# Splitting one late output store by partitions, so that eight DMA engines carry more of it than the other eight

## The chip, the cores and the metric

One Trainium2 chip, one of its cores. The metric is the device time of one execution in microseconds; the kernel before has a median of 211.49 us over five runs (210.92 to 213.69).

## What is computed

```python
batch, m, k, n = 16, 512, 1024, 768
# x: (16, 512, 1024), weight: (1024, 768), sub_value: (16, 512, 768), all float32
def reference(x, weight, sub_value):
    return (np.matmul(x, weight) - sub_value).astype(np.float32)
```

One matrix product of 8192 rows by 1024 by 768, from which a matrix of the output's shape is subtracted. In float32 the core reads 33.6 MB of `x`, 25.2 MB of `sub_value` and 3.1 MB of weights, and writes 25.2 MB.

## The kernel before, in words

**Tiling.** The 8192 rows are 64 tiles of 128 rows (`mi` from 0 to 63). Eight tiles make a superblock of 1024 rows in which partition `p` holds eight neighbouring rows (L56 to L58). So a transfer of `n` tiles is, in every one of 128 partitions, one run that is contiguous in HBM and in SBUF: n x 4096 bytes for `x`, n x 3072 bytes for `sub_value` and the output.

**Rings.** `x_ring` holds 16 tiles of `x`; `so_ring` holds 32 tiles of `sub_value`. The result of a tile is written over its `sub_value` tile in the same slot, and the store reads it there.

**Work on a tile.** ScalarE casts `x` to float16 (`cast`, L134 or L131). Of most tiles TensorE makes the transposes (L143) and ScalarE copies them out of PSUM (L150); of ten pairs of tiles VectorE does the transposes instead (L164). TensorE then does 16 matmuls of 128x384 (L176). VectorE subtracts (`finish`, L188) and writes `so_ring`.

**Order of the transfers.** All transfers are issued by SyncE (SP), on one queue, in the order of the list `TRANSFERS` (L23 to L30), written by hand. An entry is a kind (`x`, `w`, `s` for sub_value, `o` for output), a first tile and a number of tiles. `issue()` (L90) is called after every cast and every finish; it takes the next entry off the list when what it needs is done, and stops at the first that has to wait. A store `('o', at, n)` needs `finish` of all its tiles. At the end of the list of the kernel before stand six stores in a row: `('o', 32, 8)`, `('o', 40, 8)`, `('o', 48, 8)`, `('o', 56, 5)`, `('o', 61, 2)`, `('o', 63, 1)` behind the last load `('s', 56, 8)`; the last three of them finish the output.

**The code that the change touches.** One line issues a store, L119, and one a load, L121; each of them is one DMA over all 128 partitions:

```python
            here = ring[:, at % size : at % size + n]
            there = view[at // S][:, at % S : at % S + n]
            if kind == "o":
                keep(nc.sync.dma_start(out=there, in_=here))
```

Each DMA is spread over the core's 16 DMA engines, and raises its completion semaphore once for each engine that took part. The program ends (L287) when SP has seen all completions.

Of the kernel before, what the change touches and what calls it, by code (L numbers as in the profile page):

```python
# [8 lines left out]
P = 128  # L9
# [16 lines left out]
    ('x', 16, 2), ('x', 18, 6), ('s', 16, 8), ('x', 24, 8), ('s', 24, 8), ('x', 32, 8),  # L26
    ('o', 0, 8), ('x', 40, 8), ('s', 32, 8), ('o', 8, 8), ('o', 16, 8), ('s', 40, 8),
    ('x', 48, 8), ('o', 24, 8), ('s', 48, 8), ('x', 56, 8), ('s', 56, 8), ('o', 32, 8),
    ('o', 40, 8), ('o', 48, 8), ('o', 56, 5), ('o', 61, 2), ('o', 63, 1),
]  # L30


@with_exitstack
def kernel(
# [7 lines left out]
    nc = tc.nc  # L42
    keep = tc.keep_in_program_order
# [46 lines left out]
    def issue():  # L90
        while todo:
            kind, at, n = todo[0]
            span = set(range(at, at + n))
            old = {t - NX if kind == "x" else t - NSO for t in span}
            need, by = {
                "w": (set(), "o"),
                "x": ({t for t in old if t >= 0}, "cast"),
                "s": ({t for t in old if t >= 0}, "o"),
                "o": (span, "finish"),
            }[kind]  # L100
            if not need <= done[by]:
                return
            todo.pop(0)
            done[kind] |= span
            if kind == "w":

                first = NSO - 2 * (n_c - at)
                st = so_ring[:, first : first + 2]
                keep(nc.sync.dma_start(out=st, in_=w_c[at]))  # L109
                for r in range(2):  # L110
                    keep(nc.vector.tensor_copy(out=w_sb[:, at, r], in_=st[:, r]))  # L111
                continue
            ring, size, view = {
                "x": (x_ring, NX, x_s), "s": (so_ring, NSO, sub_s), "o": (so_ring, NSO, out_s)
            }[kind]
            here = ring[:, at % size : at % size + n]
            there = view[at // S][:, at % S : at % S + n]
            if kind == "o":
                keep(nc.sync.dma_start(out=there, in_=here))  # L119
            else:  # L120
                keep(nc.sync.dma_start(out=here, in_=there))  # L121

    def cast(mi):
        assert mi in done["x"]
        done["cast"].add(mi)
        x_in = x_ring[:, mi % NX]
        first = mi - mi % 2
        if first in ON_DVE:
            if mi == first:
                x16_t["pair", mi] = x16p_pool.tile([P, 2, K], F16, name="x16p_tile")  # L130
            keep(nc.scalar.copy(out=x16_t["pair", first][:, mi - first], in_=x_in))  # L131
        else:
            x16_t[mi] = x16_pool.tile([P, K], F16, name="x16_tile")
            keep(nc.scalar.copy(out=x16_t[mi], in_=x_in))  # L134
        issue()
# [48 lines left out]
    def finish(mi):  # L184
        assert mi in done["s"]
        done["finish"].add(mi)
        o = so_ring[:, mi % NSO].rearrange("p (h n) -> p h n", h=2)
        keep(nc.vector.tensor_tensor(  # L188
            out=o, in0=po_t.pop(mi)[:, :, :NS], in1=o, op=mybir.AluOpType.subtract
        ))  # L190
        issue()

    issue()


# [96 lines left out]
```

## Time and profile before

| | |
|---|---|
| median of five runs | 211.49 us (210.92 to 213.69) |
| the profiled execution | 211.42 us; its span in the profile 209.6 us |
| granted TensorE clock, mean | 0.983 |
| PE busy | 195.6 us (93%) |
| DVE busy | 134.5 us (64%) |
| ACT busy | 106.7 us (51%) |
| data queue (q1) | 5040 packets, 87.03 MB, 97.6% of 16 engines' span |
| last matmul ends, last subtraction ends | 202.0 us, 203.0 us |
| the last three stores are issued at | 194.66, 200.40 and 203.00 us |

How to read it: the span runs from the first to the last instruction that the profiler recorded; the execution's own time has 1.8 us more. All times inside the profile are counted from the start of the span. A packet is one run of one transfer on one DMA engine, or the 4-byte write with which an engine reports that its share of a transfer is done; 35 transfers x 16 engines give 560 such reports, and these are the 560 packets under 512 bytes. Two other queues carry no data of the kernel: q8 and q14 are of the kind "instruction".

### The profile page before, as it was taken

How to read it: one execution, taken by the hardware profiler on the slowest of the kernel's cores; microseconds unless marked ns; L12 is line 12 of the kernel's file. 1: busy time of each engine (PE TensorE's matmuls, PEld its weight loads, DVE VectorE, ACT ScalarE, POOL GpSimd, SP SyncE). 2: the span in 40 equal slices, each digit the busy share in tenths (PEclk: the TensorE clock that was granted, in tenths of full speed). 3: DMA queues.
4: the chain of work that ended last, by engine and by line, in shares of the span. 5: the costliest groups of instructions: out<-in, count | busy, mean ns of one | idle time of the engine just before them, and what ended most of it. 6: DMA issues, size and time to landing. Idle time of an engine off the chain costs nothing.

```text
span 209.6 us, 2950 instructions
## 1 busy us (share of the span) xinstructions
PE 195.6 (93%) x1225; PEld 127.5 (61%) x1225; DVE 134.5 (64%) x234; ACT 106.7 (51%) x109; POOL 0.7 (0%) x6
## 2 busy tenths in 40 slices
PE   7589699999999999999999999999999999999950
PEld 3246366766766666666666666666665656776620
DVE  0131332489999965999838999995398994332330
ACT  3353847938282537554464917350955243755300
POOL 1000000000000000000000000000000000000000
PEclk9969999999999999999999999999999999999996
DMA  6999999999999999999999999999999999999993
GB/s 217 423 444 424 434 421 422 450 425 430 422 464 411 417 444 439 413 428 452 411 424 431 427 435 427 441 414 419 422 441 441 435 411 427 431 439 422 424 407 131
DMA packets 5052, 87.21 MB, mean 416 GB/s; under 512 B 560, under 2 KB 560, under 8 KB 1456
## 3 DMA queue, kind: packets, MB, share of 16 engines
q1 hardware_dynamic: 5040, 87.03, 97.6%
q8 instruction: 9, 0.15, 0.3%
q14 instruction: 3, 0.02, 0.0%
HBM read 61.87 MB, written 25.17 MB: 415 GB/s over the span
## 4 chain that ended last, share of the span: by engine, by line
PE 80%; DMA 10%; DVE 5%; SPq 1%; issue 0%; DVEq 0%
PE psum_o L176 72%; DMA so_ring<-in_sub_value_dram 10%; PE psum_t L143 8%; DVE xtp_tile L164 3%; DVE so_ring L188 2%; SPq L109 1%; SPq L121 1%; DVEq L188 0%
## 5 line engine op out<-in xcount | busy, mean ns | idle before, releaser
L176 PE MATMUL psum_o<-w_sb,xt_tile 128*128 128x384 f16 x704 | 125.5, 327 | 1.7 <-DVE so_ring L188 1.7
L176 PEld LDWEIGHTS <-xt_tile 128*128 128x128 f16 x704 | 68.9, 98 | 40.0 <-issue 2.8
L188 DVE TENSOR_TENSOR so_ring<-psum_o,so_ring 128x768 f32<-128x768 f32 x64 | 60.8, 957 | 43.9 <-PE psum_o L176 27.6
L150 ACT COPY xt_tile<-psum_t 128x1024 f16<-128x1024 f16 x44 | 44.5, 1012 | 75.4 <-PE psum_t L143 74.8
L164 DVE STREAM_TRANSPOSE xtp_tile<-x16p_tile 32x256 f32<-32x256 f32 x160 | 69.7, 436 | 12.1 <-ACT x16p_tile L131 9.6
L176 PE MATMUL psum_o<-w_sb,xtp_tile 128*128 128x384 f16 x320 | 61.3, 326 | 0.3 <-DVE xtp_tile L164 0.2
L134 ACT CAST x_tile<-x_ring 128x1024 f16<-128x1024 f32 x44 | 45.6, 1047 | 8.2 <-DMA x_ring<-in_x_dram 8.2
L143 PE MATMUL psum_t<-ident,x_tile 128*128 128x128 f32 x176 | 46.1, 277 | 3.2 <-ACT x_tile L134 3.0
L176 PEld LDWEIGHTS <-xtp_tile 128*128 128x128 f16 x320 | 31.2, 98 | 14.7 <-DVE xtp_tile L164 1.0
L143 PEld LDWEIGHTS psum_t<-ident,x_tile 128*128 128x128 f32 x176 | 24.5, 142 | 14.7 <-ACT x_tile L134 3.8
L131 ACT CAST x16p_tile<-x_ring 128x1024 f16<-128x1024 f32 x20 | 20.9, 1046 | 6.9 <-DMA x_ring<-in_x_dram 6.9
L111 DVE CAST w_sb<-so_ring 128x768 f16<-128x768 f32 x8 | 4.1, 556 | 11.6 <-DMA so_ring<-in_weight_dram 11.6
L204 PE MATMUL psum_o<-idle_x,idle_w 128*128 128x512 f16 x25 | 8.5, 492 | 1.3 <-DVE idle_x L199 1.3
L204 PEld LDWEIGHTS <-idle_w 128*128 128x128 f16 x25 | 3.0, 120 | 4.7 <-issue 2.9
L134 ACT ACT_TABLE_LOAD x1 | 1.3, 1283 | 0.7 <-PEq L276 0.7
L198 DVE MEMSET idle_w<- 128x64 uint32 x1 | 0.1, 112 | 0.8 <-PEq L276 0.8
masks.py:199 POOL TENSOR_SCALAR_AFFINE_SELECT ident<-ident 128x128 f32<-128x128 f32 x1 | 0.3, 292 | 0.1
L199 DVE MEMSET idle_x<- 128x256 uint32 x1 | 0.3, 272 | 0.0
masks.py:197 POOL MEMSET ident<- 128x128 f32 x1 | 0.2, 206 | 0.3 <-POOLq L276 0.3
L276 POOL MEMSET const-uint8-127<- 128x1 uint8 x1 | 0.1, 102 | 0.0
L276 POOL MEMSET const-bfloat16-1.0<- 128x1 bf16 x1 | 0.1, 101 | 0.0
L276 POOL MEMSET const-float32-0.0<- 128x1 f32 x1 | 0.1, 98 | 0.2 <-issue 0.2
(1 smaller groups left out, 0.1 us busy)
## 6 DMA issues: line engine op xcount, KB each, us to landing
so_ring<-in_sub_value_dram SPq DMA_DIRECT2D x7, 3072.0 KB, 27.4
out_dram<-so_ring SPq DMA_DIRECT2D x7, 3072.0 KB, 30.6
x_ring<-in_x_dram SPq DMA_DIRECT2D x5, 4096.0 KB, 20.5
so_ring<-in_weight_dram SPq DMA_DIRECT2D x4, 768.0 KB, 10.7
x_ring<-in_x_dram SPq DMA_DIRECT2D x2, 1536.0 KB, 18.6
so_ring<-in_sub_value_dram SPq DMA_DIRECT2D x2, 1536.0 KB, 24.5
x_ring<-in_x_dram SPq DMA_DIRECT2D x1, 3072.0 KB, 25.2
x_ring<-in_x_dram SPq DMA_DIRECT2D x1, 2560.0 KB, 26.9
```

The costliest lines, as they stand in the source:

```text
L109: keep(nc.sync.dma_start(out=st, in_=w_c[at]))
L111: keep(nc.vector.tensor_copy(out=w_sb[:, at, r], in_=st[:, r]))
L121: keep(nc.sync.dma_start(out=here, in_=there))
L131: keep(nc.scalar.copy(out=x16_t["pair", first][:, mi - first], in_=x_in))
L134: keep(nc.scalar.copy(out=x16_t[mi], in_=x_in))
L143: keep(nc.tensor.transpose(ps_t[mi].bitcast(F32)[:, c * P : (c + 1) * P], x16_t[mi].bitcast(F32)[:, c * P : (c + 1) * P], ident,))
L150: keep(nc.scalar.copy(out=xt_t[mi], in_=ps_t.pop(mi)))
L164: keep(nc.vector.transpose(xt[b * Q : (b + 1) * Q, :, a * Q : (a + 1) * Q], x16[a * Q : (a + 1) * Q, :, b * Q : (b + 1) * Q],))
L176: keep(nc.tensor.matmul(po_t[mi][:, h, :NS], xt_t[mi][:, 2 * P * c + r : 2 * P * (c + 1) : 2], w_sb[:, c, r, h * NS : (h + 1) * NS], start ...
L188: keep(nc.vector.tensor_tensor(out=o, in0=po_t.pop(mi)[:, :, :NS], in1=o, op=mybir.AluOpType.subtract))
L204: keep(nc.tensor.matmul(idle_o[:, 0], idle_w, idle_x, start=True, stop=True))
L276: nc = _bacc.Bacc("TRN2", target_bir_lowering=False, num_devices=1)
```

## The change

The third last store takes four tiles instead of five, and an additional store takes the fifth with its neighbour: five, two and one tiles become four, two, one and one. The store of four tiles is issued as four DMAs, one after the other, over partitions 0 to 63, 64 to 71, 72 to 79, and 80 to 127. All other transfers stay single DMAs over 128 partitions. By the description that comes with the change, the first eight DMA engines carry nine runs of this store, the others seven.

```diff
     ('x', 48, 8), ('o', 24, 8), ('s', 48, 8), ('x', 56, 8), ('s', 56, 8), ('o', 32, 8),
-    ('o', 40, 8), ('o', 48, 8), ('o', 56, 5), ('o', 61, 2), ('o', 63, 1),
+    ('o', 40, 8), ('o', 48, 8), ('o', 56, 4), ('o', 60, 2), ('o', 62, 1), ('o', 63, 1),
 ]
+
+SPLIT = ('o', 56)
+PARTS = ((0, 64), (64, 72), (72, 80), (80, 128))
...
             here = ring[:, at % size : at % size + n]
             there = view[at // S][:, at % S : at % S + n]
-            if kind == "o":
-                keep(nc.sync.dma_start(out=there, in_=here))
-            else:
-                keep(nc.sync.dma_start(out=here, in_=there))
+            for lo, hi in PARTS if (kind, at) == SPLIT else ((0, P),):
+                if kind == "o":
+                    keep(nc.sync.dma_start(out=there[lo:hi], in_=here[lo:hi]))
+                else:
+                    keep(nc.sync.dma_start(out=here[lo:hi], in_=there[lo:hi]))
```

## The prediction

> **What bounds the kernel now.** I read the page's DMA rows first, then the table of windows over the tail, SP's waits, and the list of DMA issues. From the page:
>
> ```profile
> DMA  6999999999999999999999999999999999999993
> q1 hardware_dynamic: 5040, 87.03, 97.6%
> ```
>
> The DMA engines have no free slice between the first and the last. TensorE is busy for 93%, but its last matmul ends at 202.0 us and the last subtraction at 203.0, while the span ends at 209.6. The chain of waits ends in that subtraction and does not show the store behind it. The windows (after the times: five engines' busy us, PEclk, DMA share, GB/s) do:
>
> ```profile
> 203.00:204.00 1.00, 0.00 (x0) 0.00 (x0) 0.00 (x0) 0.00 (x0) 0.00 (x0) 1.00 0.94 396
> 204.00:205.00 1.00, 0.00 (x0) 0.00 (x0) 0.00 (x0) 0.00 (x0) 0.00 (x0) 1.00 0.95 390
> 205.00:206.00 1.00, 0.00 (x0) 0.00 (x0) 0.00 (x0) 0.00 (x0) 0.00 (x0) 0.89 0.58 240
> 206.00:207.00 1.00, 0.00 (x0) 0.00 (x0) 0.00 (x0) 0.00 (x0) 0.00 (x0) 0.50 0.43 172
> 207.00:208.00 1.00, 0.00 (x0) 0.00 (x0) 0.00 (x0) 0.00 (x0) 0.00 (x0) 0.50 0.05 22
> ```
>
> The queue drains in steps: all 16 engines until 205, under half of them from 206, one (0.05 is about 1/16) from 207. SP waits for that one:
>
> ```profile
> SPq L287 <- DMA out_dram<-so_ring: 5.2, 1, 5.2
> ```
>
> The three last stores land 11.1, 7.2 and 5.5 us after their issue at 194.66, 200.40 and 203.00, so at 205.8, 207.6 and 208.5:
>
> ```profile
> out_dram<-so_ring SPq DMA_DIRECT2D x1, 1920.0 KB, 11.1
> out_dram<-so_ring SPq DMA_DIRECT2D x1, 768.0 KB, 7.2
> out_dram<-so_ring SPq DMA_DIRECT2D x1, 384.0 KB, 5.5
> ```
>
> Why one engine is late: packets carry no engine number, but on an engine that never idles each starts where the last ended, so they can be followed in 16 chains. Every transfer's reports (16 of them) then come in the same order, and an engine falls back only where an "instruction" packet gets between its data. Nine packets of 16,384 B on q8 do so (at 24.2, 45.7, 67.5, 85.6, 105.8, 124.3, 145.9, 164.9, 184.9 us); the first took 1.07 us, the data run behind it 1.255 where 0.766 is usual: 1.55 us lost. They hit eight different engines in turn, the ninth the first again. Reports of the store of tiles 48 to 55, in us after the first one at 197.54:
>
> ```
> 0  0.15 0.15 0.41 0.43 0.56 | 1.80 1.88 1.95 2.03 2.05 2.17 2.39 2.45 2.57 | 3.71
> ```
>
> Six engines are early, nine late, one twice late. The last one's final packet ends at 208.16, the next engine's at 207.06. Only what these engines still have to move sets the end.
>
> [...] The trace has only full transfers, at 27.0 GB/s per engine (a run of 15,360 B each 569 ns). [...]
>
> **The change part by part.** Everything up to the subtraction of tile 59 is untouched. The DMAs rise from 35 to 39 (the last three stores become four, one of them in four DMAs), each 0.33 us of SP's time; SP does nothing else then. The first goes out after tile 59, about 3 us earlier than 194.66, into a queue which is busy with earlier stores until 197: no gain, no loss. The instruction order shows new waits, on completions of the load of x 56 (for the 48-partition part) and of the stores of tiles 32 and 40 (for 62 and 63); these landed by 170.8, 187.0 and 194.0, before the data of those stores is ready, so nothing queues behind them. If SP were late, its cover is the backlog: the last engine has work until 208.
>
> *Bytes.* Each engine moves the same total except for this store: one run of 12,288 B more on the first eight, one less on the others. A run takes 569 x 12288/15360 = 455 ns. Smaller runs cost about 4 ns each beyond that (a 3072 B run 118 ns, against 569/5 = 114), and a report 6 to 9: nine runs and four reports more come to 0.08 us on the first eight, seven and two to 0.05 on the others. Without anything else: first eight +0.54 us, others -0.40.
>
> *Ports.* [...] The cost of sharing isn't in the trace. [...] Then on the first eight: part one 4 x 0.455 = 1.82 us if the partner is away (it may be 1.8 us ahead, exactly one part) up to 3.64; parts two and three 4 x 0.455 = 1.82 each, 3.64; part four 1.37 to 1.82. Together 6.8 to 9.1 us, where four tiles by 128 partitions take 8 x 0.455 = 3.64: +3.2 to +5.5 on these engines. Since the last engine runs nearly alone, it is the group before it that sets the end. If the late group is the first eight, its rear (2.5 behind, against 3.7 for the last engine) ends 3.2 to 5.5 - 1.2 = 2.0 to 4.3 us later than the end now. If it is the other eight, the first eight hold the early ones (0.6 behind): 0.1 to 2.4 later, and more by the two of the ten late engines that must then be among them (1.9 and over behind: 1.4 to 3.7). I take the sharing as full, [...] and +3.2 us, about the middle of the case with the late ones in front and the upper half of the other.
>
> Sum: 211.42 + 3.2 = 214.6 us; the profiled execution is 0.07 under the median of the five, so no correction. The span would be 212.8.
>
> **The rivals.**
>
> *A, ports shared (58%):* above; 214.6, own range 212.9 to 215.9.
>
> *B, no port cost, the late engines are the upper eight (18%), the one of the other sign:* the last engine has one run less, 208.16 - 0.40; the next, at 207.06, ends at most 0.54 later, at 207.60, and doesn't overtake it. 211.0 us. [...] For it: engines are paced at 27.0 GB/s in loads and stores alike, which may be the engine's own limit.
>
> *C, no port cost, the late engines are the lower eight (13%):* the last engine has one run more: +0.54, 212.0 us. Nothing in the trace tells B from C; the instruction packets hit eight of 16 in turn, by number unknown.
>
> *D, the change doesn't do what it says (11%):* if the engine follows from the partition also in small transfers, [...] each engine still gets eight runs[...]. Only 0.05 to 0.08 us of packets are added: 211.5 us.
>
> **How the numbers follow.** About 1% (2.1 us) is what a measurement of this kernel can tell from no change; above 213.6 is slower, under 209.4 faster. A lies above 213.6 in some 85% of its cases: 0.58 x 0.85 = 0.49, rounded to 0.50. B, C, D and the rest of A lie within 1%: 0.50. No mechanism gains 1% (the last engine is only 1.1 us behind the next); I take 0.02 off the middle for what I haven't seen, which leaves 0.48. Range: B's 211.0 less 0.1 to A's 215.8, outside of it some 0.05 below and 0.08 above; A's own range is 212.9 to 215.9.
>
> **What would show it.** In the profile of after: packets of 12,288 B in the tail, 128 of them. If they take about 0.46 us, ports cost nothing (B, C or D); if many take 0.9 or 1.8, A. The number of reports: 39 transfers x 16, less 16 if two DMAs use eight engines only (608), or fewer if D. The last landing at 211 to 212.5 in A, 207.8 in B, 208.7 in C. In the windows after 203 the DMA share stays high in A while the GB/s fall to half. Wrong would be all of it if something before 191 us moved: tiles 0 to 59 and the loads must stand as they were, and PE must end at 202.0.

## The result and the profile after

The change makes the kernel slower by 1%: 214.39 us median over 43 runs, against 211.95 us for the kernel before in 80 runs beside it, ratio 1.0101 with a 95% interval of 1.0083 to 1.012. That is +2.1 us (211.95 x 0.0101; 1.8 to 2.5), where +3.2 was forecast. The ratio compares the fast executions alone (those within 1.5% of the fastest of their kernel), so it is smaller than the quotient of the two medians, 1.0115. The profiled execution has a span of 212.8 us, to the tenth what was forecast. That is chance: in this execution the last subtraction already ended at 203.66 us, 0.7 us later than in the profile before (202.98).

The windows over the tail of the changed kernel (after the times: busy us of five engines, PEclk, DMA share, GB/s):

```profile
203.00:204.00 1.00, 0.00 (x0) 0.00 (x0) 0.66 (x1) 0.00 (x0) 0.00 (x0) 1.00 0.99 277
204.00:205.00 1.00, 0.00 (x0) 0.00 (x0) 0.00 (x0) 0.00 (x0) 0.00 (x0) 1.00 0.98 295
205.00:206.00 1.00, 0.00 (x0) 0.00 (x0) 0.00 (x0) 0.00 (x0) 0.00 (x0) 0.67 0.92 341
206.00:207.00 1.00, 0.00 (x0) 0.00 (x0) 0.00 (x0) 0.00 (x0) 0.00 (x0) 0.50 0.78 307
207.00:208.00 1.00, 0.00 (x0) 0.00 (x0) 0.00 (x0) 0.00 (x0) 0.00 (x0) 0.50 0.75 295
208.00:209.00 1.00, 0.00 (x0) 0.00 (x0) 0.00 (x0) 0.00 (x0) 0.00 (x0) 0.50 0.30 120
209.00:210.00 1.00, 0.00 (x0) 0.00 (x0) 0.00 (x0) 0.00 (x0) 0.00 (x0) 0.50 0.11 46
210.00:211.00 1.00, 0.00 (x0) 0.00 (x0) 0.00 (x0) 0.00 (x0) 0.00 (x0) 0.50 0.10 40
```

The reader is to see two columns part: at 203 to 204 the engines are busy for 0.99 of the time and move 277 GB/s, where before 0.94 went with 396. They hold packets longer for the same bytes. And at the end not one engine is alone but between one and two (0.10 and 0.11 of 16 are 1.6 and 1.8), 2 us later than the single one of before. From the DMA rows of the page, and SP's waits:

```profile
DMA packets 5228, 87.21 MB, mean 410 GB/s; under 512 B 608, under 2 KB 608, under 8 KB 1632
```

```profile
SPq L291 <- DMA out_dram<-so_ring: 7.7, 4, 4.1
```

608 reports are 37 transfers on 16 engines and two on eight; the counts of before were 560, and the wait 5.2. The packets of the tail fit, end to start, 16 chains in which eight engines carry nine of the 128 runs of the split store and eight carry seven: four each from the part of 64 partitions, one each from the parts of eight, to the same eight engines, and three each from the part of 48. *The first eight* is below the name of those that the parts of eight use.

The packet records of the two traces say how long a run of the split store held its engine. All 128 packets of 12,288 bytes, by their duration, with two experiments told below ahead of the rest because they belong in the same table:

```
kernel                      0.46 to 0.50   over 0.50   longest   sum of 128
sizes alone (e1)                  128           0        0.49      59.0 us
after                              87          41        1.92      82.8 us
halves, 0-63 and 64-127 (e2)       77          51        1.95      82.8 us
halves, even and odd (e8)         128           0        0.49      59.0 us
```

Where all 128 are short (e1, e8), a run takes 0.46 to 0.49 us. Others take up to 1.95 us, four times that. Below, a run *meets* others when it takes longer than its bytes do alone; what it waits for is in no packet record. What the recorded texts call *shared ports* is an assumption of the author's: engines that work on neighbouring partitions at the same time hold each other up, at worst as if they had the 27.0 GB/s of one engine between them. How many engines share was assumed as well, and no trace shows a port. The experiments can show whether the choice of partitions makes the long packets.

For a measure that depends less on what an execution did earlier, the experiments below also use *the tail*: from the last report of the store of tiles 48 to 55 to the last report of all. Where the latest engine stays the latest, it is what that engine needs for the last eight tiles. Before: 7.28 us (64 runs of a tile's 3072 bytes at 0.1138 us, a fifth of 0.569, are 7.28). After: 10.85 in this profile, 9.01 in another of the same kernel (e10). It is of one execution, and where packets meet it scatters; the ratios are over many runs and decide the size.

### The profile page after: what moved, and what is told of

It is laid out like the page before. It is cut to its first block, busy times and chain, and to the rows that moved or that the text cites. A ratio compares the mean times of both kernels' runs of the same rounds, so it can differ in the third digit from the quotient of the medians.

```text
span 212.8 us, 2956 instructions
## 1 busy us (share of the span) xinstructions
PE 196.7 (92%) x1225; PEld 128.0 (60%) x1225; DVE 134.6 (63%) x234; ACT 106.5 (50%) x109; POOL 0.7 (0%) x6
## 4 chain that ended last, share of the span: by engine, by line
PE 88%; DMA 4%; ACT 2%; issue 1%; DVE 0%; SPq 0%
PE psum_o L180 77%; PE psum_t L147 9%; DMA x_ring<-in_x_dram 4%; ACT x_tile L138 1%; PE psum_o L208 1%; ACT xt_tile L154 0%; DVE so_ring L192 0%; SPq L112 0%; SPq L125 0%
## 5 line engine op out<-in xcount | busy, mean ns | idle before, releaser
L180 PE MATMUL psum_o<-w_sb,xt_tile 128*128 128x384 f16 x704 | 126.9, 329 | 0.3 <-DVE so_ring L192 0.3
```

The source lines that it names most:

```text
L180: keep(nc.tensor.matmul(po_t[mi][:, h, :NS], xt_t[mi][:, 2 * P * c + r : 2 * P * (c + 1) : 2], w_sb[:, c, r, h * NS : (h + 1) * NS], start ...
```

## The experiments

**The sizes alone (e1)**: four, two, one and one tiles, no split.

```diff
-PARTS = ((0, 64), (64, 72), (72, 80), (80, 128))
+PARTS = ((0, 128),)
```

> The new sizes alone: the store of four tiles stays one DMA over 128 partitions. Shared ports and uneven load both say no change against before (within 0.2 us), all 12,288-byte packets at 0.46 us, last landing near 208.2 in the profile. If the loss came from the sizes or from the earlier issue, it stands here already: about +2.1 us.

Measured: ratio to before 1.0001 (0.9973 to 1.003), the tail 7.32 us. The new sizes and the earlier issue cost nothing that this can tell (0.3%); the loss is in the split.

**Two halves, the load even (e2)**

```diff
-PARTS = ((0, 64), (64, 72), (72, 80), (80, 128))
+PARTS = ((0, 64), (64, 128))
```

> The store of four tiles in two DMAs, partitions 0 to 63 and 64 to 127: every engine carries eight runs, as before. Shared ports: many packets at 0.9 us and more, +1 to +3 us against before. Uneven load as the only cause: no change (within 0.2 us), packets at 0.46 us.

Measured: 1.0042 (1.0014 to 1.007), +0.9 us, just under the stated +1; the tail 9.24, +1.96. All its 37 transfers go over 16 engines (592 reports), and by the four runs that a part of 64 partitions gave each engine in the change, every engine carries eight runs; so uneven load can't be the cause of this loss. Its windows:

```profile
203.00:204.00 1.00, 1.00 (x8) 0.61 (x7) 0.00 (x0) 0.00 (x0) 0.00 (x0) 1.00 1.09 283
204.00:205.00 1.00, 0.60 (x4) 0.14 (x2) 0.37 (x1) 0.00 (x0) 0.00 (x0) 1.00 1.11 307
```

Full share, 283 GB/s: the same sign as in the change.

**Nine and seven runs by another cut (e3)**

```diff
-PARTS = ((0, 64), (64, 72), (72, 80), (80, 128))
+PARTS = ((0, 8), (8, 16), (16, 128))
```

> The same nine and seven runs as in the change, by three DMAs: partitions 0 to 7, 8 to 15, 16 to 127. [...] Shared ports: on the first eight 2 x 1.37 = 2.7 us more, of which the early engines have up to 1.9 + 1.1 to spare, so between 0 and +1 us against before. Uneven load as the only cause: the same as the change, about +2.1 us.

Measured: 1.0121 (1.0072 to 1.0169), +2.6 us; the tail 8.93, +1.65. A miss: no cheaper than the change. 33 of its 128 packets took over 0.5 us. Followed engine by engine (each packet starts where the last one ended, as in the prediction), only 2 of these 33 are among the 16 runs of the two small parts, and 31 among the 112 of the third. So it is the other way round than estimated: the small parts hardly met, the large one did. That its runs would not meet had been assumed. Alone, this run can't tell meetings from uneven load.

**Ten and six runs without a meeting in the small parts (e4, and e11 again on another chip)**, on the store of two tiles. Here and in the later runs with three numbers to a part, the line that issues takes the step as well; that line is not shown.

```diff
-SPLIT = ('o', 56)
-PARTS = ((0, 64), (64, 72), (72, 80), (80, 128))
+SPLIT = ('o', 60)
+PARTS = ((0, 32, 4), (1, 32, 4), (2, 32, 4), (3, 32, 4), (32, 128, 1))   # from, to, step
```

> No split of the store of four tiles; the store of two tiles goes in four DMAs of eight partitions, each with partitions four apart [...], and one over partitions 32 to 127: ten runs of 6144 bytes on the first eight engines, six on the others, which is 2 x 0.228 = 0.46 us more and less, the same shift as in the change. Shared ports with the late engines in the upper eight: -0.4 us against before. With the late engines in the lower eight: +0.5. Uneven load as the cause of the loss, or the number of small DMAs: +2 us as in the change.

> The strided parts on the store of two tiles once more: if the gain of 0.4% over the kernel before was more than the scatter of that series, it is -0.2 to -0.6% again (0.4 to 1.2 us); the last engine should again be one of the upper eight.

Measured: 0.9961 (0.9936 to 0.9986) and 0.9947 (0.99 to 0.9995); the tail 6.85 and 6.86, 0.43 us under before. By the ratios that is 0.8 and 1.1 us, with intervals that hold 0.46. Moving 0.46 us of work from the last engine brings about that in the tail, and four small DMAs more do no harm here. It isn't free: the 128 runs of this store sum to 33.7 us in both, against 30.0 in e1, since runs of the part of 96 partitions still meet; but the tail shows none of it on the engine that ends last. This version is faster than both kernels. Its reports also tell which engines, the early or the late ones, are the first eight. The ones of the store of four tiles came, behind 203.07, at

```
all 16:              0 .05 .17 .22 .29 .69 1.05 1.62 1.75 1.86 1.91 1.95 2.35 2.59 2.76 3.34
first eight, part 1: 0 .05 .20 .22              1.63 1.76      1.88 1.96   (+ one run, 0.23)
```

Four early ones, four late ones; the latest four, and the last of all, are in the other eight.

**The twin of that with neighbours (e5)**: same DMAs, same bytes per engine, other partitions.

```diff
-PARTS = ((0, 32, 4), (1, 32, 4), (2, 32, 4), (3, 32, 4), (32, 128, 1))
+PARTS = ((0, 8, 1), (8, 16, 1), (16, 24, 1), (24, 32, 1), (32, 128, 1))
```

> The twin of the run before it with the strided parts: the same store of two tiles, the same five DMAs, the same ten and six runs of 6144 bytes, only that each DMA of eight partitions takes eight neighbours[...]. Shared ports: the first eight engines lose up to 4 x 3 x 0.234 = 2.8 us in step; spread over an early and a late half, about 4 x 0.234 to 4 x 3 x 0.234, 0.9 to 2.8 us on the late ones, which have 0.4 + 1.4 us to spare: between 0 and +1.4 us against before, +0.4 to +1.8 against the strided twin. Uneven load or small DMAs as the cause of the loss: the same time as the strided twin (-0.8 us against before).

Measured: 1.0009 (0.9981 to 1.0037). The gain is gone, by 0.48% or 1.0 us between the two ratios. That meetings took it isn't shown. In the one profiled execution (214.66 us; the series has a median of 212.47) the runs of this store sum to 33.7 us, just as in e4, and the mean of the reports moves by 0.23, 0.28 and 0.24 us from one small part to the next (e4: 0.23, 0.23 and 0.24), so the small parts hardly met. Its tail of 7.71 has another reason: of the engines that report the store of four tiles last, the second is one of the first eight, only 0.14 us ahead of the last. With 0.47 us more it becomes the last one, and the end moves by 0.33 the wrong way. The twins differ in SP's time too: 0.28 to 0.39 us per small DMA here, 0.63 to 0.77 in e4. So this pair leaves the cause open.

**Ten and six runs of four tiles (e6)**

```diff
-SPLIT = ('o', 60)
+SPLIT = ('o', 56)
```

> The strided parts on the store of four tiles: ten and six runs of 12,288 bytes, so 0.92 us more on the first eight and 0.92 less on the others. Shared ports and the last engine in the upper eight: that engine gains 0.9, the late ones of the first eight (2.0 behind, against 3.3 to 3.6) come 0.9 later and end with it: -0.6 to -0.9 us against before, 12,288-byte packets mostly at 0.46. Uneven load as the cause of the loss: slower than before, by twice the 0.46 of the change.

Measured: 1.0002 (0.9966 to 1.0039), the tail 7.63. A miss in size, with a reason in the reports: the late ones among the first eight were 2.2 us behind, the last engine 3.5. With 0.91 more and 0.91 less they pass it by, and even without a meeting the end moves by 2.2 + 0.91 - 3.5 = -0.4; the store's sum of 65.9 us against 59.0 shows that the part of 96 partitions did have meetings, which used that up.

**Halves in the middle of the kernel (e7)**, the tail as before:

```diff
-            if kind == "o":
+            if (kind, at) == ("o", 16):
+                for lo, hi in ((0, 64), (64, 128)):
+                    keep(nc.sync.dma_start(out=there[lo:hi], in_=here[lo:hi]))
+            elif kind == "o":
...
```

> The tail as before; the store of tiles 16 to 23, in the middle of the kernel, goes in two DMAs, partitions 0 to 63 and 64 to 127. Each engine still carries eight runs of 24,576 bytes. Shared ports: part of these 128 runs takes 1.8 us and more instead of 0.91, and as no engine is idle at any time the loss stays: +2 to +5 us against before. If only the tail is sensitive (uneven load, late engines): no change.

Measured: 1.0334 (1.0272 to 1.0396), 218.88 us against 212.02, more than the +2 to +5 expected. The windows of this run, and then the same ones of the kernel before:

```profile
118.00:124.00 6.00, 6.00 (x40) 3.93 (x39) 5.81 (x12) 2.61 (x4) 0.00 (x0) 1.00 1.08 348
124.00:130.00 6.00, 6.00 (x40) 3.87 (x39) 5.81 (x12) 3.92 (x5) 0.00 (x0) 1.00 0.93 257
130.00:136.00 6.00, 6.00 (x41) 4.02 (x39) 5.81 (x12) 2.49 (x3) 0.00 (x0) 1.00 0.92 313
136.00:144.00 8.00, 4.46 (x29) 2.78 (x28) 0.78 (x3) 2.90 (x3) 0.00 (x0) 1.00 1.03 439
```

```profile
118.00:124.00 6.00, 6.00 (x40) 3.93 (x39) 5.81 (x12) 2.61 (x4) 0.00 (x0) 1.00 1.00 430
124.00:130.00 6.00, 6.00 (x40) 3.89 (x39) 5.81 (x12) 3.92 (x5) 0.00 (x0) 1.00 1.01 433
130.00:136.00 6.00, 6.00 (x41) 4.00 (x39) 5.81 (x12) 2.61 (x3) 0.00 (x0) 1.00 1.06 455
136.00:144.00 8.00, 8.00 (x52) 5.10 (x51) 7.67 (x14) 2.96 (x4) 0.00 (x0) 1.00 0.97 403
```

One store of 3 MB in two halves takes the bandwidth from 433 to 257 GB/s; from 136 on TensorE waits for loads that come late (4.46 of 8 us busy). Packets between 112 and 137 us hold their engines 77.5 us longer than at 0.912 each, 4.8 us per engine, and the spread between first and last engine grows from 2.2 to 9.1 us, which fits a loss above the mean. Its tail is 7.30 us: nothing at the end is needed for a loss.

**Halves by parity (e8)**: the test of e2 with other partitions.

```diff
-PARTS = ((0, 64), (64, 72), (72, 80), (80, 128))
+PARTS = ((0, 128, 2), (1, 128, 2))   # from, to, step
```

> The store of four tiles in two DMAs as in the run by halves, but the even partitions in one and the odd ones in the other[...]. If an engine takes four neighbours of the list (0, 2, 4, 6 and so on), [...] still pairs in step, +0.5 to +2 us against before. If the shares are dealt out by port, no packet over 0.5 us, and no change against before. Two DMAs as such as the cause: the same as by halves (+0.9 us) with all packets at 0.46.

Measured: 0.9994 (0.9959 to 1.0029), the tail 7.30, no packet over 0.5 us. Same number of DMAs, same count of 64 partitions, all 16 engines in every transfer (592 reports) and the same bytes as in e2; only which partitions each DMA takes is different. The loss of e2, 0.9 us by the ratios and 2 us in its tail, is gone.

```profile
203.00:204.00 1.00, 0.00 (x0) 0.00 (x0) 0.38 (x1) 0.00 (x0) 0.00 (x0) 1.00 0.97 402
204.00:205.00 1.00, 0.00 (x0) 0.00 (x0) 0.00 (x0) 0.00 (x0) 0.00 (x0) 1.00 0.88 356
```

**The twin of the change (e9), and the change beside it (e10)**: DMAs of 64, 8, 8 and 48 partitions in both.

```diff
-PARTS = ((0, 64), (64, 72), (72, 80), (80, 128))
+PARTS = ((0, 128, 2), (1, 33, 4), (3, 35, 4), (33, 128, 2))   # from, to, step
```

> The twin of the change: the store of four tiles in four DMAs of 64, 8, 8 and 48 partitions, nine runs on the first eight engines and seven on the others, exactly as in the change; only which partitions they are differs: 0, 2, ... 126; then 1, 5, ... 29; then 3, 7, ... 31; then 33, 35, ... 127. [...] Shared ports: few packets over 0.5 us (only in the part of 48), the end 0 to 0.5 us before that of the kernel before, so 2 us and more under the change. Uneven load or the number of DMAs: +2.1 us as the change itself.

> The change itself beside its twin on the same chip: +2.1 us against before, 40 or so of its 128 packets of 12,288 bytes at 0.5 to 1.95 us. Should the twin be as slow as this run, shared ports are out.

Measured: the twin 1.0006 (0.9974 to 1.0039), the change 1.0117 (1.0047 to 1.0188). Packets over 0.5 us: 7 of 128 in the twin, 41 in the change. With the same shapes and bytes on the same chip the loss is there with neighbours and not there with spread partitions. The stated gain of up to 0.5 us isn't seen in the twin; its part of 48 partitions still has meetings (up to 1.06 us).

**The strided parts with the old sizes (e12)**: five, two and one tiles, `SPLIT = ('o', 61)`, parts as in e4.

> The same strided parts with the stores of five, two and one tiles of the kernel before; the store of tiles 61 and 62 is the one that is split. The shift of 2 x 0.234 us from the last engine is the same, so the same -0.4 us; but the DMAs are issued later (200 to 203 us, five in a row at 0.4 to 0.8 us each), so the last store goes out about 0.4 us later, which matters for the early engines only. If the new sizes were a part of the gain, this one shows less.

Measured: 1.0007 (0.9971 to 1.0044), the tail 8.31: the gain is lost. The expectation counted SP's time as a matter for early engines only. SP took 0.77, 0.65, 0.63 and 0.63 us for the four small DMAs from 203.39 on; all eight engines report each within 0.7 us, at 205.3, 206.1, 206.7 and 207.4, so they sit waiting for the next one:

```profile
205.00:206.00 1.00, 0.00 (x0) 0.00 (x0) 0.96 (x1) 0.00 (x0) 0.00 (x0) 1.00 0.29 117
206.00:207.00 1.00, 0.00 (x0) 0.00 (x0) 0.00 (x0) 0.00 (x0) 0.00 (x0) 1.00 0.28 114
207.00:208.00 1.00, 0.00 (x0) 0.00 (x0) 0.00 (x0) 0.00 (x0) 0.00 (x0) 0.64 0.83 252
```

In e4 the split store goes out from 199.94 on, 3.5 us earlier, and the backlog covers that. So the new sizes are a part of e4's gain.

## Why the prediction was right, and where it was not

*The bound.* Right: only the latest DMA engine's remaining work sets the end. Where no run of the tail meets another, it is 7.28, 7.32, 7.30 and 7.30 us in four kernels (before, e1, e7, e8), the time of 64 runs.

*The engines and the reports.* Right as to their number: 608 reports; the parts of eight partitions get eight each. Rival D is out. Which eight they are by number no trace shows; the same eight come back in every small part (e4).

*The ports.* What is shown is that the choice of partitions decides: e2 against e8 (1.0042 and 0.9994, 51 packets over 0.5 us and none) and e10 against e9 (1.0117 and 1.0006, 41 and 7) differ in nothing but which partitions a DMA takes, and the loss goes with the neighbours. From 203 to 204 us e2 moves 283 GB/s where e8 moves 402. The upper bound taken, that engines which share have the rate of one between them, was an estimate; measured are 0.46 us alone and 0.5 to 1.95 in company. One rival was not tested: each partition has its own rows in HBM, so in every one of these pairs the addresses there change along with the partitions. Where the long packets wait, at a port or elsewhere, was not shown.

*Bytes, and rivals B and C.* The last engine is in the other eight (the upper ones of the prediction) in the traces of e4 and e11, so B had its place right there, and the -0.40 us of it is seen: the tail is 0.43 shorter. B failed as a forecast of this change, in which the long runs do cost. C is out by the same traces for these executions; e5's, with a late engine in each group, shows that the place is not always so clear.

*The size: +3.2 forecast, +2.1 measured.* The direction and the wait stood; the terms of the sum did not, and errors of both signs went some way to cancel. The packets of the profile after, followed engine by engine, give each part's mean time per engine; the column "given" is the prediction's estimate:

```
part of the store          given for the first eight   first eight   other eight
one, partitions 0-63            1.82 to 3.64              2.41          2.01
two, 64-71                      1.82                      0.67           -
three, 72-79                    1.82                      0.85           -
four, 80-127                    1.37 to 1.82              2.17          2.30
all                             6.8 to 9.1                6.10          4.31
```

The reports agree where they can be told apart: from those of part two to those of part three 0.84 us, and 0.84 again in e10. The step that failed is "parts two and three 4 x 0.455 = 1.82 each": the first eight aren't in step. Their reports of the store before part one fall into four within 0.7 us and four that are 1.5 to 2.6 us behind the first, so the eight are seldom at one part together, and only 7 of these 16 runs took over 0.5 us. Part four was priced too low: 22 of its 48 runs did. The case analysis "late group in front, or in the other eight" was wrong in the same way as parts two and three: it is half and half. That the middle of its two cases came within about 1 us of the measured loss is in part luck.

*Who ends last.* Right in kind: the last report of part three in the profile after is at 204.44, and three runs more can't end before 205.81; only two reports of part four are later than 205.41 (207.14 and 208.17). So an engine of the first eight is one of the two that end last. By the packets both are, with ends at 211.6 and 210.5 us; the engine that was twice interrupted is done at 208.4.

*SP's time.* "Each 0.33 us" was wrong: the four parts took 0.52, 1.26, 0.98 and 1.16 us to issue. It was covered here, as named there, by the backlog: the last of the four was issued by 196.37, and the first engine was done with the store before them at 197.73. e12 shows what it costs without that.

## What to carry to other kernels

When a DMA takes only some of the partitions, look at which ones it takes before counting how many engines it uses: halves of 64 neighbours cost this kernel 0.9 us at the end and 7 us in the middle, where halves of alternate partitions cost nothing at the end (in the middle they weren't tried). One transfer of 128 partitions was never slower here than two of 64: contiguous halves lost (1.0042 at the end, 1.0334 in the middle), alternate ones were level with the single DMA (0.9994).

If a queue is full to the end, shifting runs away from its latest engine is worth about the shift (0.43 us of tail here), if the small DMAs that do it are issued well ahead (e12). Whether they must also take spread partitions is open: with neighbours the gain was gone (e5), but the trace doesn't show why.

## What the runs showed of the hardware that was not expected

- In two contiguous halves, packets took up to 1.95 us, 4.2 times 0.46, where the estimate had at most doubled them (3.64 for four runs that take 1.82 alone). By parity none took over 0.49. Which partitions go to which engine was not found out.
- SP's time to issue a DMA of eight partitions differed with which these are: the first one of a series took 0.77 us with partitions four apart (e4, e6, e11, e12) and 0.35 with eight neighbours (e3, e5), against 0.33 for one of 128 partitions. In the change, behind the part of 64 partitions, the two DMAs of eight neighbours took 1.26 and 0.98 us.
- Which engine is latest, and by how much, differs from one execution to another: in e4 and e11 the last is 0.58 and 1.02 us behind the next in the reports of the store of four tiles, in e5 0.14. Whether the packets of 16,384 bytes on q8 come to the same engines in each execution was not tested.
